# Mean over the rows of an 8192 x 8192 matrix: one add in halves, two groups at double width, and another first block for TensorE

## The chip, the cores and the metric

The kernel runs on one core of a Trainium2 chip. The metric is the device time of one execution in microseconds (us); of several runs the median is given. A profiled execution also has a span, which is the stretch of time that the trace covers; the time is somewhat longer than the span.

A core has engines that run side by side, each with its own queue of instructions: TensorE (in the profile PE, its weight loads PEld), VectorE (DVE), ScalarE (ACT), GpSimd (POOL) and SyncE (SP). Transfers are made by 16 DMA engines, to which an instruction of some engine's queue hands the work (such an instruction has a q behind the engine's name: SPq, ACTq). Engines wait for one another and for transfers by semaphores.

## The reference

```python
def setup_inputs():
    return {"x": np.random.randn(8192, 8192).astype(np.float32)}

def reference(x):
    return np.mean(x, axis=0)
```

268.4 MB are read, and 8192 sums, scaled by 1/8192, are written: 32 KB.

## The kernel before

The 8192 rows are taken as G = 64 groups of 128 rows; a group fills the 128 partitions with 8192 columns each (4 MB). The kernel has six such buffers in `bufs`: buffers 0 to 3 take loads in turn, buffer 4 is `both` and buffer 5 is `acc`, the accumulator. A "block" is F = 512 columns, so a group has 16 blocks.

**Loads.** All are issued by SyncE in a fixed order (L54), each when its buffer is free: 2 blocks of group 60 into `early`, groups 0 to 3 into buffers 0 to 3 in one transfer, groups 4 and 5 into `both` and `acc`, 4 blocks of group 63 into `early`, and then, from group 6 on, two groups in one transfer of 8 MB, in turn into buffers 0 and 1 and into 2 and 3. (`load_rows` with n groups takes n neighbouring rows to one partition; the sum over rows doesn't mind.) After group 59 come 14 blocks of group 60, all of 61 and 62, and group 63 in four parts: blocks 4 to 7, blocks 0 to 3, the columns B to Z, and the columns A to B. A is block 12, Z the end of block 15, and B lies 640 columns behind A.

**VectorE's adds** (L74, helper `add`). The first two are of double width, 128 x 16384: buffers 2 and 3 += buffers 0 and 1, then buffers 4 and 5 += buffers 2 and 3. Then `acc` += `both`. From there the loop takes two groups a step (g = 6, 8, ..., 58): `both` = one loaded buffer + the other, which frees these two for the next load, and `acc` += `both`. Behind the loop, `acc` takes blocks 0 to 13 of group 60 in one add of 7168 columns, and blocks 12 to 15 of group 61 in an add of 2048.

An add that needs a transfer doesn't wait for it alone: a no-op on ScalarE or GpSimd (L77) waits for the transfer and for the add ahead, and the add waits for the no-op. Which of the two engines has the no-op follows from the number of adds so far: `len(adds) % 8 > 1` gives ScalarE, else GpSimd. A warm-up copy on ScalarE (L95), with the table load that goes with it, stands behind the three first adds in the program, and has no no-op ahead of it on ScalarE.

**GpSimd** adds the two `early` pieces into `acc` behind the steps g = 24 and 32 (L107); the next add into `acc` waits for that through a no-op. At the end it adds the last blocks of group 62 into `acc`, in two parts (L122).

**TensorE** (L149) sums over the 128 partitions, by a matmul with a matrix of ones scaled by 1/8192, 32 columns wide. Four blocks lie in the four column groups of the array, and their sums in four quarters of a PSUM bank; three banks hold blocks 0 to 3, 4 to 7 and 8 to 11, and `most` and `last` hold the columns B to Z and A to B. Each block of float32 shows as two matmul records in the trace. The order is that in which `sums` was filled: `r61` (group 61) blocks 0 to 11, `acc` blocks 0 to 11, `r62` blocks 0 to 11, `r63` blocks 4 to 7, `most` from `acc`, `r63` blocks 0 to 3, `last` from `acc`, `most` and `last` from `r63`.

**The end.** ScalarE copies the banks (L163) and VectorE copies `last` (L179); five stores (L166) on SyncE and ScalarE write the result.

The two places of the order that the change touches:

```python
    for lo, hi, loaded in [(0, 14, 14), (12, 16, 16)]:
        row = bufs[:, (g + 2) % 4, :]
        dma = load(row[:, :loaded * F], rows(g)[:, :loaded * F])
        cols = slice(lo * F, hi * F)
        add(acc[:, cols], acc[:, cols], row[:, cols], [dma])
        g += 1
...
    blocks(r61, 0, 12)
    blocks(acc, 0, 12)
    blocks(r62, 0, 12)
```

Of the kernel before, what the change touches and what calls it, by code (L numbers as in the profile page):

```python
# [9 lines left out]
def kernel(  # L10
# [5 lines left out]
    nc = tc.nc  # L16
# [3 lines left out]
    F = 512  # L20
# [9 lines left out]
    bufs = sb.tile([P, U, N], f32, name="bufs")  # L30
    both = bufs[:, U - 2, :]
    acc = bufs[:, U - 1, :]
# [20 lines left out]
    def load(dst, src):  # L53
        ins = tc.keep_in_program_order(nc.sync.dma_start(out=dst, in_=src)).ins  # L54
        k = len(loads)
        over = loads[k - 8:k - 6] if k >= 8 and k % 2 == 0 else []
        tc.declare_no_dep(ins, group="loads", keep=over, reason="the reader of the buffer waited")
        for o in over:
            tc.add_manual_dep(ins, o.name, sync, reason="covers the next load too")
        tc.add_to_no_dep_group("loads", ins)  # L60
        loads.append(ins)
        return ins

    def rows(g, n=1):
        return x[g * P:(g + n) * P, :]

    def load_rows(g, u, n):
        return load(bufs[:, u:u + n, :], rows(g, n).rearrange("(p j) c -> p j c", j=n))
# [2 lines left out]

    def add(dst, a, b, dmas):

        ins = nc.vector.tensor_add(out=dst, in0=a, in1=b).ins  # L74
        if dmas and adds:
            waiter = nc.scalar if len(adds) % 8 > 1 else nc.gpsimd
            nop = joins[waiter] = tc.keep_in_program_order(waiter.nop()).ins  # L77
            for o in dmas + adds[-1:]:
                tc.add_manual_dep(nop, o.name, sync, reason="the no-op waits")
            for group in ("loads", "adds"):  # L80
                tc.declare_no_dep(ins, group=group, reason="the no-op waited")
            tc.add_manual_dep(ins, nop.name, sync, reason="waits for both at once")
        elif adds:
            tc.declare_no_dep(ins, group="loads", reason="the add ahead waited")
        tc.declare_no_dep(ins, group="early", reason="the no-op waited, or the add behind it")
        tc.add_to_no_dep_group("adds", ins)
        adds.append(ins)

    load(early[:, 4 * F:], rows(G - 4)[:, 14 * F:])
    first, second = load_rows(0, 0, 4), load_rows(4, 4, 2)  # L90
    load(early[:, :4 * F], rows(G - 1)[:, 8 * F:12 * F])
    add(bufs[:, 2:4, :], bufs[:, 2:4, :], bufs[:, 0:2, :], [first])
    add(bufs[:, 4:6, :], bufs[:, 4:6, :], bufs[:, 2:4, :], [second])
    add(acc, acc, both, [])
    tc.keep_in_program_order(nc.scalar.copy(out=warm[:], in_=ones[:]))  # L95
    ahead = []
    g = 6
    while g < G - 4:
        u = (g + 2) % 4
        dma = load_rows(g, u, 2)  # L100
# [3 lines left out]
        if g in (24, 32):  # L104
            lo, hi, at = (0, 4, 8) if g == 24 else (4, 6, 14)
            cols = slice(at * F, (at + hi - lo) * F)
            ins = tc.keep_in_program_order(nc.gpsimd.tensor_add(  # L107
                out=acc[:, cols], in0=acc[:, cols], in1=early[:, lo * F:hi * F])).ins
# [1 line left out]
            ahead = [ins]  # L110
        g += 2

    for lo, hi, loaded in [(0, 14, 14), (12, 16, 16)]:
        row = bufs[:, (g + 2) % 4, :]
        dma = load(row[:, :loaded * F], rows(g)[:, :loaded * F])
        cols = slice(lo * F, hi * F)
        add(acc[:, cols], acc[:, cols], row[:, cols], [dma])
        g += 1
    r61, r62, r63 = [bufs[:, (g + 1 + j) % 4, :] for j in range(3)]
    load(r62, rows(g))  # L120
    for cols in [slice(B, Z), slice(A, B)]:
        joined = tc.keep_in_program_order(nc.gpsimd.tensor_add(  # L122
            out=acc[:, cols], in0=acc[:, cols], in1=r62[:, cols])).ins
# [6 lines left out]
    def blocks(row, lo, hi):  # L130
        for i in range(lo, hi):
            sums.append((banks[i // 4], i % 4, row[:, i * F:(i + 1) * F]))

    def spread(dst, row, lo, hi):
        n = (hi - lo) // 4
        for q in range(4):
            sums.append((dst, q, row[:, lo + q * n:lo + (q + 1) * n]))

    blocks(r61, 0, 12)
    blocks(acc, 0, 12)  # L140
    blocks(r62, 0, 12)
    blocks(r63, 4, 8)
    spread(most, acc, B, Z)
# [4 lines left out]
    for n, (dst, q, cols) in enumerate(sums):  # L148
        summed = tc.keep_in_program_order(nc.tensor.matmul(  # L149
            out=dst[32 * q:32 * q + 32, :],  # L150
# [71 lines left out]
```

## Time and profile before

| | |
|---|---|
| three runs | 627.96, 629.09 and 629.38 us; median 629.09 |
| profiled execution | 628.06 us |
| its span | 626.1 us |
| VectorE busy | 525.6 us, 60 instructions |
| of these 55 adds of 128 x 8192 | 8744 ns each |
| 2 adds of 128 x 16384 | 17226 ns each |
| the add of 128 x 7168 and that of 128 x 2048 | 7624 and 2292 ns |
| TensorE busy | 15.5 us, 120 records |
| read from HBM | 268.44 MB, 429 GB/s over the span |

All times inside the profile are us from the start of the span. "L74" is line 74 of the kernel. The chain of waits is the work that ended last, followed back from the last instruction: start, duration, engine, tile and line. In a row of instructions, what stands in brackets is the idle time of the engine ahead of them, and who ended it. The windows view gives the busy time of each engine in a stretch, then the clock that TensorE was granted (1.00 is full speed), the mean share of the 16 DMA engines, and GB/s; a DMA packet is counted whole in the window in which it starts, so that a share over 1 can stand beside one of 0.

### The profile page before, as it was taken

The page shows a single profiled execution, that of the slowest core. Times are in us where ns is not written, and L with a number is a line of the kernel's source. Part 1 is how long each engine was busy: PE and PEld are TensorE (multiplying, and loading weights), DVE is VectorE, ACT ScalarE, POOL GpSimd, SP SyncE. Part 2 cuts the span into 40 slices and gives each one's busy share as a digit, 9 for nine tenths or more (in the row PEclk, how much of TensorE's full clock was granted, in tenths as well). Part 3 has the DMA queues.
Part 4 walks back from the last instruction along what each step waited for, and adds up shares of the span by engine and source line. Part 5 has one row for each costly group of instructions (what it writes and reads, how often), then busy time and mean ns, then how long its engine had stood idle before and what let it go on. Part 6 is the DMA issues. An engine that isn't in the chain of part 4 may idle for free.

```text
span 626.1 us, 465 instructions
## 1 busy us (share of the span) xinstructions
PE 15.5 (2%) x120; PEld 4.3 (1%) x120; DVE 525.6 (84%) x60; ACT 3.7 (1%) x6; POOL 12.1 (2%) x10
## 2 busy tenths in 40 slices
PE   0000000000000000000000000000000000000036
PEld 0000000000000000000000000000000000000002
DVE  0028999999888998889998889888898888998892
ACT  0000000000000000000000000000000000000001
POOL 0000000000000000020000100000000000000003
PEclk9999999999999999999999999999999999999998
DMA  9999999999999999999999999999999999999997
GB/s 377 461 402 429 442 469 402 469 402 469 402 469 402 465 406 456 414 419 452 406 465 402 469 402 469 402 469 402 469 402 469 402 465 406 431 440 410 427 435 305
DMA packets 5642, 268.50 MB, mean 429 GB/s; under 512 B 628, under 2 KB 636, under 8 KB 1032
## 3 DMA queue, kind: packets, MB, share of 16 engines
q1 hardware_dynamic: 5624, 268.46, 99.2%
q8 instruction: 1, 0.02, 0.0%
q10 hardware_dynamic: 16, 0.01, 0.0%
q14 instruction: 1, 0.01, 0.0%
HBM read 268.44 MB, written 0.03 MB: 429 GB/s over the span
## 4 chain that ended last, share of the span: by engine, by line
DMA 57%; DVE 31%; another core or an unknown queue 10%; PE 2%; issue 0%; ACTq 0%; POOL 0%; POOLq 0%
DMA bufs<-in_x_dram 57%; DVE bufs L74 31%; PE bank L149 1%; PE most L149 0%; PE last L149 0%; ACTq L77 0%; DVE tail L179 0%; POOL ready L40 0%; POOL ones L37 0%; POOLq L77 0%; POOLq L206 0%
## 5 line engine op out<-in xcount | busy, mean ns | idle before, releaser
L74 DVE TENSOR_TENSOR bufs<-bufs 128x8192 f32<-128x8192 f32 (+3 forms) x59 | 525.3, 8903 | 89.6 <-DMA bufs<-in_x_dram 43.1
L149 PE MATMUL bank<-bufs,ones 128*32 128x512 f32 x88 | 13.7, 779 | 607.8 <-DMA bufs<-in_x_dram 605.6
L107 POOL TENSOR_TENSOR bufs<-bufs,early 128x2048 f32<-128x2048 f32 (+1 forms) x2 | 6.8, 3415 | 347.7 <-DVE bufs L74 347.7
L122 POOL TENSOR_TENSOR bufs<-bufs 128x1408 f32<-128x1408 f32 (+1 forms) x2 | 4.7, 2372 | 259.8 <-DMA bufs<-in_x_dram 259.8
L149 PEld LDWEIGHTS bank<-bufs,ones 128*32 128x32 f32 x88 | 3.5, 137 | 616.7 <-issue 613.3
L179 DVE COPY tail<-last 128x160 f32<-128x160 f32 x1 | 0.3, 325 | 8.4 <-PE last L149 8.4
L163 ACT COPY bufs<-bank 128x512 f32<-128x512 f32 x3 | 1.8, 585 | 618.9 <-PE bank L149 618.9
L149 PE MATMUL most<-bufs,ones 128*32 128x352 f32 x16 | 1.5, 459 | 0.0
L95 ACT ACT_TABLE_LOAD x1 | 1.3, 1283 | 0.7 <-PEq L206 0.7
L149 PE MATMUL last<-bufs,ones 128*32 128x160 f32 x16 | 0.9, 305 | 0.0
L163 ACT COPY bufs<-most 128x352 f32<-128x352 f32 x1 | 0.5, 452 | 0.0
L149 PEld LDWEIGHTS most<-bufs,ones 128*32 128x32 f32 x16 | 0.4, 109 | 0.7 <-issue 0.6
L149 PEld LDWEIGHTS last<-bufs,ones 128*32 128x32 f32 x16 | 0.4, 109 | 1.2 <-DMA bufs<-in_x_dram 0.6
L95 ACT COPY warm<-ones 128x32 f32<-128x32 f32 x1 | 0.2, 218 | 0.0
L40 POOL TENSOR_TENSOR ready<-ones 128x1 f32<-128x1 f32 x1 | 0.2, 193 | 0.1
L37 POOL MEMSET ones<- 128x32 f32 x1 | 0.1, 124 | 0.3 <-POOLq L206 0.3
L206 POOL MEMSET const-float32-0.0<- 128x1 f32 x1 | 0.1, 98 | 0.2 <-issue 0.2
L206 POOL MEMSET const-bfloat16-1.0<- 128x1 bf16 x1 | 0.1, 101 | 0.0
L206 POOL MEMSET const-uint8-127<- 128x1 uint8 x1 | 0.1, 101 | 0.0
L206 POOL MEMSET const-float32-1.0<- 128x1 f32 x1 | 0.1, 98 | 0.0
## 6 DMA issues: line engine op xcount, KB each, us to landing
bufs<-in_x_dram SPq DMA_DIRECT2D x2, 4096.0 KB
bufs<-in_x_dram SPq DMA_DIRECT2D x1, 3584.0 KB
bufs<-in_x_dram SPq DMA_DIRECT2D x2, 1024.0 KB, 23.3
early<-in_x_dram SPq DMA_DIRECT2D x1, 1024.0 KB, 62.7
bufs<-in_x_dram SPq DMA_DIRECT2D x1, 704.0 KB, 24.5
early<-in_x_dram SPq DMA_DIRECT2D x1, 512.0 KB
bufs<-in_x_dram SPq DMA_DIRECT2D x29, 29.9
bufs<-in_x_dram SPq DMA_DIRECT2D x1, 320.0 KB, 24.8
```

What stands on the lines that cost most here:

```text
L37: nc.gpsimd.memset(ones[:], 1.0 / M)
L40: nc.gpsimd.tensor_add(out=ready[:], in0=ones[:, 0:1], in1=ones[:, 1:2]))
L74: ins = nc.vector.tensor_add(out=dst, in0=a, in1=b).ins
L95: tc.keep_in_program_order(nc.scalar.copy(out=warm[:], in_=ones[:]))
L107: ins = tc.keep_in_program_order(nc.gpsimd.tensor_add(out=acc[:, cols], in0=acc[:, cols], in1=early[:, lo * F:hi * F])).ins
L122: joined = tc.keep_in_program_order(nc.gpsimd.tensor_add(out=acc[:, cols], in0=acc[:, cols], in1=r62[:, cols])).ins
L149: summed = tc.keep_in_program_order(nc.tensor.matmul(out=dst[32 * q:32 * q + 32, :], lhsT=ones[:], rhs=cols, start=all((d is dst, k) != (T ...
L163: return tc.keep_in_program_order(nc.scalar.copy(out=dst, in_=src)).ins
L179: ended = nc.vector.tensor_copy(out=tail[:], in_=last[:]).ins
L206: nc = _bacc.Bacc("TRN2", target_bir_lowering=False, num_devices=1)
```

## The change

Three things change. Groups 6 and 7, which lie in buffers 0 and 1, are no longer the first step of the loop: they are added at double width onto buffers 4 and 5 by one add, ahead of the add of `both` into `acc`; the loop begins with group 8. The add of group 60's blocks 0 to 13 becomes two of 3584 columns, blocks 0 to 6 and 7 to 13. TensorE's order begins with blocks 0 to 6 of `acc`, then takes `r61`, then blocks 7 to 11 of `acc`. VectorE's adds are now kept in program order. The number of adds stays 59, and in the loop each step's first add has an even number instead of an odd one. All loads keep their order and sizes. The no-op for groups 6 and 7 stands ahead of the warm-up copy and its table load on ScalarE; the no-ops behind the two `early` adds of GpSimd move from GpSimd to ScalarE.

```diff
     def add(dst, a, b, dmas):
 
-        ins = nc.vector.tensor_add(out=dst, in0=a, in1=b).ins
+        ins = tc.keep_in_program_order(nc.vector.tensor_add(out=dst, in0=a, in1=b)).ins
         if dmas and adds:
             waiter = nc.scalar if len(adds) % 8 > 1 else nc.gpsimd
             nop = joins[waiter] = tc.keep_in_program_order(waiter.nop()).ins
...
     add(bufs[:, 2:4, :], bufs[:, 2:4, :], bufs[:, 0:2, :], [first])
     add(bufs[:, 4:6, :], bufs[:, 4:6, :], bufs[:, 2:4, :], [second])
+    add(bufs[:, 4:6, :], bufs[:, 4:6, :], bufs[:, 0:2, :], [load_rows(6, 0, 2)])
     add(acc, acc, both, [])
     tc.keep_in_program_order(nc.scalar.copy(out=warm[:], in_=ones[:]))
     ahead = []
-    g = 6
+    g = 8
     while g < G - 4:
         u = (g + 2) % 4
         dma = load_rows(g, u, 2)
...
-    for lo, hi, loaded in [(0, 14, 14), (12, 16, 16)]:
+    for parts, loaded in [([(0, 7), (7, 14)], 14), ([(12, 16)], 16)]:
         row = bufs[:, (g + 2) % 4, :]
-        dma = load(row[:, :loaded * F], rows(g)[:, :loaded * F])
-        cols = slice(lo * F, hi * F)
-        add(acc[:, cols], acc[:, cols], row[:, cols], [dma])
+        dmas = [load(row[:, :loaded * F], rows(g)[:, :loaded * F])]
+        for lo, hi in parts:
+            cols = slice(lo * F, hi * F)
+            add(acc[:, cols], acc[:, cols], row[:, cols], dmas)
+            dmas = []
         g += 1
...
+    blocks(acc, 0, 7)
     blocks(r61, 0, 12)
-    blocks(acc, 0, 12)
+    blocks(acc, 7, 12)
     blocks(r62, 0, 12)
     blocks(r63, 4, 8)
```

## The prediction

> **What bounds the kernel now.** I read the page first: busy shares, slices, queues.
>
> ```profile
> PE 15.5 (2%) x120; PEld 4.3 (1%) x120; DVE 525.6 (84%) x60; ACT 3.7 (1%) x6; POOL 12.1 (2%) x10
> DMA  9999999999999999999999999999999999999997
> q1 hardware_dynamic: 5624, 268.46, 99.2%
> ```
>
> The queue of the loads is busy for 99.2% of the span. VectorE (DVE), at 84%, has slack, and the chain of waits shows how much:
>
> ```profile
> 62.40 0.04 POOLq L77
> ...
> 62.46 17.24 DVE bufs L74
> ...
> 79.72 8.70 DVE bufs L74
> ...
> 88.51 8.70 DVE bufs L74
> ...
> 161.58 0.04 ACTq L77
> ...
> 200.28 0.03 ACTq L77
> ```
>
> From 161.58 on a landing releases VectorE, every 38.70 us for two pairs of groups: 19.35 us a pair, against 2 x 8.70 us of adds. Counting back in steps of 19.35 from 161.58, groups 8 and 9 land at 103.53 and groups 6 and 7 at 84.18. (Forwards: groups 4 and 5 had landed at 62.40, the 1 MB of `early` behind them is an eighth of a pair, 2.42, and 62.40 + 2.42 + 19.35 = 84.17.) So no load was late, from the first on. What can change the time is a load issued too late, or work behind the last landing. For the second, the end of the chain and TensorE's timeline:
>
> ```profile
> 604.88 7.63 DVE bufs L74
> ...
> 612.56 7.91 PE bank L149 x56
> ...
> 622.19 0.59 PE most L149 x8
> ...
> 622.01 0.77 PE L149 MATMUL most<-bufs,ones 128*32 128x352 f32 x8
> 622.75 0.11 PEld L149 LDWEIGHTS last<-bufs,ones 128*32 128x32 f32 x2 [0.61 <-DMA bufs<-in_x_dram]
> ```
>
> The chain goes through the add of group 60 and TensorE, but the last row says that TensorE's last weights waited for a transfer, until 622.75. The `most` blocks ahead, started at 622.01 and taking 0.59 by the chain, were through at 622.60. So the last landing sets the end, and TensorE is 0.15 us short of setting it. From 622.75 to 626.1 stay 3.35 us that the change doesn't touch.
>
> **The change, part by part.** The tail first.
>
> VectorE's half add: the 7168-wide add takes 7.624 us and the 2048-wide one 2.292, so an element per partition costs 5.332 / 5120 = 1.041 ns and 3584 cost 2.292 + 1536 x 0.001041 = 3.89. Started at 604.88, the first half ends at 608.77; the second, 0.02 behind it as in the chain, at 612.68, 0.17 later than today. The 2048-wide add then ends near 615.07; GpSimd, which follows, is held by the landing of group 62 until 615.45, so 0.38 us of cover takes the 0.17; without it GpSimd's first add would move 0.17 for matmuls that come 3 us behind it.
>
> TensorE: a block of 512 is two matmul records, and four blocks run side by side; I call four records a pass. By the timeline's weight loads a pass takes 0.85 us at first (606.43, 607.28, 608.13) and 0.43 later (617.28, 617.71, 618.14). The granted clock by stretches:
>
> ```profile
> 606.27:609.68 3.41, 3.41 (x20) 0.92 (x16) 3.41 (x1) 0.00 (x0) 0.00 (x0) 1.00 0.91 394
> 609.68:613.09 3.41, 1.24 (x16) 0.24 (x12) 3.31 (x2) 0.00 (x0) 0.00 (x0) 1.00 0.87 375
> 613.09:616.50 3.41, 3.41 (x24) 0.87 (x20) 1.80 (x1) 0.00 (x0) 1.05 (x1) 0.50 1.00 423
> 616.50:619.90 3.40, 3.40 (x40) 1.01 (x36) 0.00 (x0) 0.22 (x1) 3.40 (x2) 1.00 0.99 410
> ```
>
> (Columns: stretch, length, busy PE, PEld, DVE, ACT, POOL, granted clock, DMA.) A stretch of 3.41 us that TensorE filled is followed by full clock, one with 1.24 of 3.41 busy by half clock. (In the first stretch the passes of 0.85 say half clock, though the column has 1.00.) Today's 14 passes from 612.56 to the end of `r63`'s first part, at full clock 14 x 0.43 = 6.02, and half of 3.41 lost to the half clock, 1.71, give 620.29, where the timeline has the next matmuls. Changed: TensorE starts at 608.77 + 0.06 = 608.83, not at 605.60. Seven blocks make two groups (4 + 3), `r61` three, and blocks 7 and 8 to 11 two more, as block 7 stands alone: 14 passes where today there are 12. With the eight of `r62` and `r63` that is 22 x 0.43 = 9.46. If the stretches lie as today, half clock lasts from 608.83 to 613.09 and costs 2.13: the same point is reached at 620.42, 0.13 later. The waiting 0.15 us takes that. Block 7 isn't reached before 608.83 + 10 x 0.43 = 613.13, behind the second half's 612.68. Sum of the tail: 0.0.
>
> Where will the boundaries lie? In quarter-microsecond windows the granted clock falls at 613.09 and rises at 616.50; neither these nor 609.68 fits TensorE's starts at 605.60 and 612.56, so the rows don't tell how they lie to a start at 608.83.
>
> The Trainium skill, "TensorE: Matmul & The Clock Gate", Part 1, says outright that the window of 3.4 us is free-running and not started by the kernel. The 3.41 above agrees; by the page the 0.13 would be a draw, anywhere between the ends that follow.
>
> By the rows: full clock comes at the end of a filled stretch, so at best the half clock lasts 1.24 us of part-filled stretch (more than 1.24 busy is needed), costing 0.62, and at worst 2 x 3.41 = 6.82, costing 3.41. The point today at 620.29 then lies between 618.91 and 621.70; behind it come 0.59, 0.86, 0.27 and 0.59 (chain), so the last blocks could start between 621.2 and 624.0, against 622.75 for the last landing: the tail costs 0.0 to +1.3, and nothing up to 4.3 us of half clock. The runs of before have the same uncertainty, with a gap from 610.4 to 612.56. I take 0.0, the alignment of the one execution that is shown.
>
> The start. Groups 6 and 7 were added alone, at 88.51, and their buffers were free at 97.21. One double-width add takes 17.23, not 2 x 8.70 + 0.02: VectorE is spared 0.19. But it stands ahead of the add into the accumulator and must wait for groups 6 and 7: VectorE now idles from 79.70 to 84.18 + 0.06 = 84.24, ends at 101.47, and the buffers come free 4.26 us later. The load of groups 10 and 11, issued at 97.23, goes out at 101.49. Queued behind the waiting add are the accumulator's adds: groups 8 and 9 are added at 110.2 to 118.9 (106.0 to 114.7 today), their buffers' next load still 3.5 us ahead of its need. VectorE gains 1.93 us per pair and is level by 181. When does the transfer of groups 8 and 9 let go? Packets are counted at their start:
>
> ```profile
> 102.50:102.75 0.25, 0.00 (x0) 0.00 (x0) 0.25 (x1) 0.00 (x0) 0.00 (x0) 1.00 1.22 524
> 102.75:103.00 0.25, 0.00 (x0) 0.00 (x0) 0.25 (x1) 0.00 (x0) 0.00 (x0) 1.00 7.89 3408
> 103.00:103.25 0.25, 0.00 (x0) 0.00 (x0) 0.25 (x1) 0.00 (x0) 0.00 (x0) 1.00 0.61 262
> 1.75:2.00 0.25, 0.00 (x0) 0.00 (x0) 0.00 (x0) 0.25 (x1) 0.00 (x0) 1.00 1.56 147
> 3.50:3.75 0.25, 0.00 (x0) 0.00 (x0) 0.00 (x0) 0.00 (x0) 0.00 (x0) 1.00 3.80 1622
> ```
>
> Groups 10 and 11 begin at 102.5 to 103.25, most near 102.88: 1.39 us after the new issue (5.65 us after the old). An issue's lead is seen at the kernel's start only: the first went out at 0.74 and moved data from 1.75, 1.0 us; the second, at 1.19, had its large packets from about 3.6, 2.4 us, though behind the first. By 1.0 nothing is lost, by 2.4 it is 1.0 us, and all that follows is late by it. I take 1.5, nearer to the first row because the second contains another transfer: +0.1.
>
> The skill's "DMA: Bandwidth & Descriptors", Latency and other measured facts, speaks against the change: it gives HBM access as 0.2 us on average and 2 us at high load. No run here shows a load issued to a nearly empty queue mid-kernel. An estimate by that page alone, 1.0 + 1.8 = 2.8 us of lead, would lose 1.4 us.
>
> At no cost: ScalarE's table load and copy (1.28 + 0.22) move behind the no-op at 84.2; ScalarE's next no-op is needed at 110.2. Without that cover VectorE would wait 1.5. The no-ops of groups 26 and 34 move from GpSimd to ScalarE: 0.04 against 0.05 in the chain, under VectorE's 1.93 of idle. SP issues the same loads in the same order.
>
> Sum: 0.0 + 0.1 against the profiled execution, 628.06 with 2 us around its 626.1; the median, 1.03 higher, becomes 629.2.
>
> **Rivals.** No change, 629.2, is the forecast.
>
> Slower: TensorE sets the end. It starts 3.23 us later and does two passes more, so when a boundary falls just ahead of 608.83 and nearly a filled stretch is needed, the last blocks are ready 1.3 us behind the last landing: 630.4. For: the end is 0.15 us from TensorE. Against: it takes most of a second stretch at half clock. It costs from 4.3 us of half clock on, and the full price needs 6.8.
>
> Slower or inside 0.2%: the queue runs dry before groups 10 and 11. It costs from 1.4 us of lead on; at 2.4 us 630.1, at 2.7 us 630.4. For: the margin shrinks from 5.65 us to 1.4. Against: the row of 1.0.
>
> Faster: the median of before is 1.03 over the profiled execution. If that is a late TensorE (the gap behind 610.4 can leave two stretches short of busy, so 5 to 6.8 us at half clock behind 612.56 where today it is 3.41, some 1.3 us more), the unbroken run of matmuls removes it: 629.09 - 1.3 = 627.8. For: the gap. Against: one execution is shown, and there the gap costs nothing.
>
> That the change doesn't do what it says: TensorE is to be busy without a break, yet it begins 3.23 us later, on an add rather than on a landing. If the pause is only moved ahead, nothing comes of it; the time is the forecast's.
>
> **How the numbers follow.** The forecast has 0.53; TensorE late 0.17; the dry queue 0.12, half of it over 0.2%; the faster rival 0.18. A measurement of this kernel can tell about 0.2%, 1.26 us, from no change. So slower is 0.17 + 0.06 = 0.23, same 0.53 + 0.06 = 0.59, faster 0.18. The range leaves out about half of each outer case: from 627.7, just under the faster rival, to 630.6, just over TensorE late. The forecast's own range is 628.5 to 630.2: 0.7 below by the scatter of the three runs (half of 1.4), above by the dry queue's 1.0.
>
> **What would show it.** Groups 10 and 11 landing at 122.9 (steps right) or up to 124 (queue dry); DMA slices without a hole after 101.5; halves of 3.89 us; TensorE's first matmul at 608.8 and no gap until `r63`; the last weights still waiting for a DMA. Wrong if VectorE's wait moves ahead of a landing after 181, or if the time behind the last landing isn't 3.35 us.

## The result and the profile after

The changed kernel takes 631.25 us (median of 8 runs, 630.38 to 633.04) against 629.12 for the one before: ratio 1.0040, 95% interval 1.0027 to 1.0054. It is slower by 2.1 us, and the forecast of no change was wrong. The profiled execution took 631.26 us, its span is 629.3, 3.2 us longer than the 626.1 of before.

First the page of the changed kernel, its busy line and the queue of the loads:

```profile
PE 14.3 (2%) x120; PEld 4.3 (1%) x120; DVE 525.5 (84%) x60; ACT 3.7 (1%) x6; POOL 12.1 (2%) x10
q1 hardware_dynamic: 5624, 268.46, 98.9%
```

Engines do the same work as before, and the queue is busy for 98.9% of the span instead of 99.2%. 0.3% of 629 us is 1.9 us of 16 engines, so the loads are the place to look. The chain of waits of the changed kernel (start, duration, what):

```profile
60.41 23.85 DMA bufs<-in_x_dram
...
84.32 17.24 DVE bufs L74
...
101.58 8.70 DVE bufs L74
...
136.61 28.16 DMA bufs<-in_x_dram
164.77 0.03 ACTq L77
...
203.47 0.03 ACTq L77
...
608.11 3.90 DVE bufs L74
...
612.14 11.49 PE bank L153 x80
```

The double-width add starts at 84.32, on the landing of groups 6 and 7, and ends at 101.56 (84.24 and 101.47 were computed). Then the landing that releases VectorE stands at 164.77 where it stood at 161.58: all of the 3.2 us is lost by 165 us, and nothing behind it: 203.47 is 38.70 later, the same step as before, and the add of group 60 starts at 608.11 instead of 604.88, 3.23 later. The end keeps its length too. TensorE's timeline and SyncE's issues in the changed kernel:

```profile
101.57 0.33 SPq L54 DMA_DIRECT2D bufs<-in_x_dram  x1
625.97 0.13 PEld L153 LDWEIGHTS last<-bufs,ones 128*32 128x32 f32 x4 [0.63 <-DMA bufs<-in_x_dram]
```

The last weights wait for a DMA again, 3.22 us later than at 622.75; from there to the end are 3.3 us (3.35 before). Now the place: the load of groups 10 and 11 goes out at 101.57. The windows view of before, then of the changed kernel; the last two columns are the share of the DMA engines and GB/s, counted where a packet starts:

```profile
102.50:103.00 0.50, 0.00 (x0) 0.00 (x0) 0.50 (x1) 0.00 (x0) 0.00 (x0) 1.00 4.55 1966
103.00:103.50 0.50, 0.00 (x0) 0.00 (x0) 0.50 (x1) 0.00 (x0) 0.00 (x0) 1.00 0.30 131
103.50:104.00 0.50, 0.00 (x0) 0.00 (x0) 0.50 (x1) 0.00 (x0) 0.00 (x0) 1.00 0.00 0
```

```profile
102.50:103.00 0.50, 0.00 (x0) 0.00 (x0) 0.50 (x1) 0.00 (x0) 0.00 (x0) 1.00 3.32 1180
103.00:103.50 0.50, 0.00 (x0) 0.00 (x0) 0.50 (x1) 0.00 (x0) 0.00 (x0) 1.00 1.08 393
103.50:104.00 0.50, 0.00 (x0) 0.00 (x0) 0.50 (x1) 0.00 (x0) 0.00 (x0) 1.00 0.00 0
104.00:104.50 0.50, 0.00 (x0) 0.00 (x0) 0.50 (x1) 0.00 (x0) 0.00 (x0) 1.00 0.39 131
104.50:105.00 0.50, 0.00 (x0) 0.00 (x0) 0.50 (x1) 0.00 (x0) 0.00 (x0) 1.00 0.76 262
105.50:106.00 0.50, 0.00 (x0) 0.00 (x0) 0.50 (x1) 0.00 (x0) 0.00 (x0) 1.00 4.37 1573
```

Such rows can be counted. A large packet is 65.5 KB, so 1966 GB/s for 0.5 us are 15 packets, and 131 are one: before, all 16 engines begin the new load within a microsecond. Their mean duration is share x 16 x 0.5 / packets: 4.55 x 8 / 15 = 2.43 us. In the changed kernel 1180 + 393 make 12 packets in the same microsecond; the other engines begin 1.3 us and more later, one between 104.0 and 104.5, two in the next half microsecond, the fourth from 105.5 on (nothing starts between 105.0 and 105.5). And the 12 take (3.32 + 1.08) x 8 / 12 = 2.93 us each instead of 2.43; so do the packets that start from 105.5 to 106 (4.37 x 8 / 12 = 2.91). The first of these, alone in a narrow window, is the fourth late engine's, as no packet of the 12 has ended by then:

```profile
105.50:105.58 0.08, 0.00 (x0) 0.00 (x0) 0.08 (x1) 0.00 (x0) 0.00 (x0) 1.00 2.42 819
```

It takes 2.42 x 16 x 0.08 = 3.10 us. So 12 engines lose some 1.0 us over two packets. The four late ones lose 1.3 us and more by idling and some 0.6 on the packet that follows; the last of them lets go of the load before between 102.8 and 103.2, by the trace's packets, and starts at 105.5, which makes 2.3 to 2.7 us, and 0.7 on its packet: 3.0 to 3.4, the 3.2 of the landing. Every load is divided evenly among the 16, and its landing waits for the last of them.

### The profile page after: what moved, and what is told of

The parts are those of the page before. It is cut to its first block, busy times and chain, and to the rows that moved or that the text cites. A ratio compares the mean times of both kernels' runs of the same rounds, so it can differ in the third digit from the quotient of the medians.

```text
span 629.3 us, 465 instructions
## 1 busy us (share of the span) xinstructions
PE 14.3 (2%) x120; PEld 4.3 (1%) x120; DVE 525.5 (84%) x60; ACT 3.7 (1%) x6; POOL 12.1 (2%) x10
## 3 DMA queue, kind: packets, MB, share of 16 engines
q1 hardware_dynamic: 5624, 268.46, 98.9%
## 4 chain that ended last, share of the span: by engine, by line
DMA 67%; DVE 30%; PE 2%; issue 0%; ACTq 0%; SPq 0%; POOLq 0%
DMA bufs<-in_x_dram 67%; DVE bufs L74 30%; PE bank L153 2%; PE most L153 0%; PE last L153 0%; ACTq L77 0%; SPq L54 0%; DVE tail L183 0%; POOLq L77 0%
## 5 line engine op out<-in xcount | busy, mean ns | idle before, releaser
L96 ACT ACT_TABLE_LOAD x1 | 1.3, 1283 | 84.3 <-DMA bufs<-in_x_dram 84.3
```

## The experiments

**The change in two halves.** First the tail alone, in the kernel before:

```diff
+    blocks(acc, 0, 7)
     blocks(r61, 0, 12)
-    blocks(acc, 0, 12)
+    blocks(acc, 7, 12)
```

with group 60 in two adds, as in the change.

> Before, with the halves of group 60 and TensorE's new order alone; groups 6 and 7 as before. Theory (the transfers ran dry before groups 10 and 11, and that is the whole loss): the time of before, ratio 0.999 to 1.001, last weights waiting for the last landing near 622.7. Rival (TensorE, which starts later and does two passes more, makes the loss): 1.003 to 1.005, without a wait of the last weights for a DMA.

Then the start alone:

```diff
+    add(bufs[:, 4:6, :], bufs[:, 4:6, :], bufs[:, 0:2, :], [load_rows(6, 0, 2)])
     add(acc, acc, both, [])
...
-    g = 6
+    g = 8
```

> Before, with groups 6 and 7 added at double width alone (the no-op for group 61 is kept on ScalarE). Theory: the whole loss, ratio 1.003 to 1.005, and the landing that releases VectorE near 164.8 instead of 161.6. Rival (the loss is at the tail): 0.999 to 1.001.

The tail alone: 628.87 us, ratio 0.9995 (0.9987 to 1.0003). Its last weights wait for a DMA, 0.7 us later than in the kernel before; that is taken up below:

```profile
623.44 0.16 PEld L152 LDWEIGHTS last<-bufs,ones 128*32 128x32 f32 x8 [0.61 <-DMA bufs<-in_x_dram]
```

The start alone: 630.97, ratio 1.0027 (1.0018 to 1.0037), a little under what was expected. The chain of waits with the start alone:

```profile
84.25 17.24 DVE bufs L74
...
136.55 27.86 DMA bufs<-in_x_dram
164.41 0.04 ACTq L77
...
203.47 0.03 ACTq L77
```

Its landing of 164.41 is 2.8 us late, and the next, at 203.47, is 3.2 late, as in the changed kernel: the loss is at the start, and the rival that TensorE makes it falls.

**Keep the add, take away the empty queue.** In the changed kernel a small load goes behind groups 8 and 9 instead of to the head:

```diff
-    load(early[:, 4 * F:], rows(G - 4)[:, 14 * F:])
...
         dma = load_rows(g, u, 2)
+        if g == 8:
+            load(early[:, 4 * F:], rows(G - 4)[:, 14 * F:])
```

> The changed kernel, with the 0.5 MB load of group 60 moved from the head of the loads to behind groups 8 and 9. The double-width add stays; groups 6 and 7 land 1.2 us sooner, so the load of groups 10 and 11 is issued near 100.3, and the queue holds the same bytes until 102.9: a lead of 2.5 us instead of 1.3. Theory (only the empty queue costs): the time of before, 0.998 to 1.001, if 2.5 us of lead is enough; part of the loss if not. Rival (the double-width add costs by itself, by the later adds behind it): 1.003 to 1.005 as in the changed kernel.

628.64 us, ratio 0.9997 (0.9987 to 1.0007), with everything else of the change in it. Its windows at the same place:

```profile
102.50:103.00 0.50, 0.00 (x0) 0.00 (x0) 0.50 (x1) 0.00 (x0) 0.00 (x0) 1.00 2.98 1270
103.00:103.50 0.50, 0.00 (x0) 0.00 (x0) 0.50 (x1) 0.00 (x0) 0.00 (x0) 1.00 2.81 1212
```

By the view of its chain the release at the place of 161.58 is at 161.87. The double-width add by itself costs nothing.

**The late issue without the change.** The kernel before, with an add on a dead tile, of four sizes, ahead of the add of groups 6 and 7 (and the adds kept in program order, as in the change):

```diff
+        if g == 6:
+            tc.keep_in_program_order(nc.vector.tensor_add(
+                out=both[:, :4000], in0=both[:, :4000], in1=both[:, :4000]))
         add(both, bufs[:, u, :], bufs[:, u + 1, :], [dma])
```

> Before, with one extra add of 4000 columns in place on the dead tile both, 4.3 us, ahead of the add of groups 6 and 7. Nothing else of the change is in it; the buffers come free at 101.5 as in the changed kernel. Theory (the late issue costs, by whatever delays it): ratio 1.003 to 1.005. Rival (the order or width of the adds): 0.999 to 1.001, as VectorE has slack.

> As the run with the extra add of 4000 columns, with 3500: 3.8 us, the load of groups 10 and 11 issued near 101.0, a lead of 1.9 us. It looks for the lead that is enough, between 1.4 (loss) and 2.3 (no loss). If the lead needed is that of the kernel's first load (1.0 to 1.6 us from issue to first packets): no loss, 0.999 to 1.001. If some engines get their descriptors later than that: part of the loss, 1.001 to 1.003.

> The same with 5120 columns, 5.5 us: issue near 102.6, a lead of 0.2 us, 1.2 us less than with 4000. If the loss is the lateness of the issue and nothing more, it grows by that 1.2 us, to 1.0045 (some 3.0 us). If an engine that has run dry pays a price of its own that covers the lateness, it stays near 1.003.

> The same with 7040 columns, 7.5 us: issue near 104.7, 1.8 us behind the first engine that lets go, so all 16 engines run dry. By lateness alone, counted from the run of 4000 columns: 1.8 + 3.2 = 5 us, 1.008; by a price of restarting of some 2 us for each engine on top of the gap of 1.8: 1.006 to 1.007.

The issue as the trace has it, the lead to 102.88, where most engines let go in the kernel before, and the landing that stands at 200.28 in the chain of the kernel before:

| columns | issue | lead | landing | time | ratio, interval |
|---|---|---|---|---|---|
| none (before) | 97.23 | 5.65 | 200.28 | 629.18 and 628.75 | 1 |
| 3500 | 101.18 | 1.70 | 200.89 | 629.15 | 1.0013 (1.0003 to 1.0023) |
| 4000 | 101.44 | 1.44 | 202.82 | 630.91 | 1.0026 (1.0016 to 1.0036) |
| 5120 | 102.70 | 0.18 | 202.12 | 630.55 | 1.0031 (1.0020 to 1.0041) |
| 7040 | 104.62 | -1.74 | 203.84 | 632.51 | 1.0062 (1.0048 to 1.0075) |

(4000 columns ran beside 629.18, the others beside 628.75.) The landing, from one execution each, has the loss of the loads at this place alone; the times also hold what happens later, of which two things are told below. An issue as late as that of the changed kernel costs 2.5 us at the landing, most of the changed kernel's 3.2, with none of its other edits. The loss isn't the lateness: from a lead of 1.44 to one of 0.18 the ratio hardly moves and the landing comes 0.7 us earlier; only with 7040 columns both grow. The windows of the run with 5120, then of that with 7040:

```profile
103.50:104.00 0.50, 0.00 (x0) 0.00 (x0) 0.50 (x1) 0.00 (x0) 0.00 (x0) 1.00 5.56 1835
104.00:104.50 0.50, 0.00 (x0) 0.00 (x0) 0.50 (x1) 0.00 (x0) 0.00 (x0) 1.00 0.71 262
```

```profile
105.00:105.50 0.50, 0.00 (x0) 0.00 (x0) 0.50 (x1) 0.00 (x0) 0.00 (x0) 1.00 0.00 0
105.50:106.00 0.50, 0.00 (x0) 0.00 (x0) 0.50 (x1) 0.00 (x0) 0.00 (x0) 1.00 5.95 1966
106.00:106.50 0.50, 0.00 (x0) 0.00 (x0) 0.50 (x1) 0.00 (x0) 0.00 (x0) 1.00 0.36 131
```

In both, all 16 engines have run dry and start together. With 7040 columns they do so 0.9 to 1.9 us after the issue at 104.62, and the first packets take 5.95 x 8 / 15 = 3.17 us. Taking 105.8 for their start, they wait 2.9 us and lose 0.74 on the first packet: 3.7, and the landing is 3.56 late. With 5120, taking 103.8, they wait 0.9 and lose 0.7 (6.27 x 8 / 16 = 3.14 us a packet): 1.6, and the landing is 1.84 late. So where all run dry the price is the wait and slow first packets. Where only some do, those come late: in the changed kernel up to 3.9 us behind the issue, while the other 12 had begun by 1.9. In the profiled executions this was the dearer case, 2.5 and 3.2 us with leads of 1.44 and 1.31, against 1.8 with one of 0.18. Why some engines get their work that late, and why the first packets are slow, wasn't found.

**The empty queue in another place.** In the changed kernel the 1 MB load of group 63 behind groups 8 and 9, in place of the small one:

> The changed kernel, with the 1 MB load of group 63 (not the 0.5 MB of group 60) moved to behind groups 8 and 9. The load of groups 10 and 11 then has a lead near 3.8 us, but that of groups 6 and 7, issued at 60.4 when the first add ends, loses the 2.4 us of transfer that stood ahead of it, and has 1.4 us. Theory (an empty queue costs wherever it comes): the loss is back, 1.002 to 1.005, with the late engines from 62 us on and none at 103. Rival (the place or the double add costs): as with the other early load, 0.999 to 1.001.

629.62 us, ratio 1.0014 (1.0005 to 1.0023); its times run from 628.54 to 630.22. The profile is of the fastest of these. Its windows, where groups 6 and 7 begin:

```profile
61.50:62.00 0.50, 0.00 (x0) 0.00 (x0) 0.00 (x0) 0.00 (x0) 0.00 (x0) 1.00 5.20 1966
62.00:62.50 0.50, 0.00 (x0) 0.00 (x0) 0.12 (x1) 0.00 (x0) 0.00 (x0) 1.00 0.37 131
```

No engine is late here, but the first packets take 5.20 x 8 / 15 = 2.77 us instead of 2.42, and the release at the place of 161.58 is at 162.06. By the times the loss is partly back, at a place that the change didn't touch; how large it is differs from one execution to the next, and late engines at this place were not seen.

**More lead.** The small load and half of the other behind groups 6 and 7:

```diff
+    load(early[:, :2 * F], rows(G - 1)[:, 8 * F:10 * F])
...
     add(bufs[:, 4:6, :], bufs[:, 4:6, :], bufs[:, 0:2, :], [load_rows(6, 0, 2)])
+    load(early[:, 2 * F:4 * F], rows(G - 1)[:, 10 * F:12 * F])
+    load(early[:, 4 * F:], rows(G - 4)[:, 14 * F:])
```

> The changed kernel, with the 0.5 MB load of group 60 and the second half of the 1 MB load of group 63 (now two loads of 0.5 MB) moved to behind groups 6 and 7. The load of groups 10 and 11 then has a lead near 4 us, that of groups 6 and 7 one of 2.6. If the empty queue is the whole loss, and the tail's change by itself takes away the upper group of times of the kernel before (a late last store, 1.1 us): 628.0 to 628.6, below both kernels, ratio 0.998 to 0.9995. If the tail's change brings nothing: 0.9995 to 1.0005, with two groups of times as before.

Neither came: 630.13 us, ratio 1.0025 (1.0013 to 1.0036), and in its chain the release at the place of 161.58 is at 162.96. Its windows, where groups 6 and 7 begin:

```profile
62.00:62.50 0.50, 0.00 (x0) 0.00 (x0) 0.50 (x1) 0.00 (x0) 0.00 (x0) 1.00 2.16 819
62.50:63.00 0.50, 0.00 (x0) 0.00 (x0) 0.50 (x1) 0.00 (x0) 0.00 (x0) 1.00 0.72 262
```

The slow packets are back at this place: 262 GB/s for 0.5 us are two packets, and they take 0.72 x 8 / 2 = 2.88 us each. The load was issued at 59.30, at least 2.2 us ahead. So 2.2 us and more wasn't enough here, with two more loads issued right behind, where 2.3 was enough above. The lead that is needed is no single number; 5.65 us lost nothing.

**What hid in the tail's result.** The tail alone came out level, yet the view of its chain has one long step (from 480 us on), and so has another profile of it:

```profile
479.90 30.66 DMA bufs<-in_x_dram
...
519.34 29.92 DMA bufs<-in_x_dram
```

It has 60 adds instead of 59. The kernel before with one more add on the dead tile, of 32 columns:

> Before, with one more instruction on VectorE alone: an add of 32 columns in place on the dead tile both, ahead of the add of groups 6 and 7; its own time is under 0.2 us and VectorE has slack. If 60 adds instead of 59 bring a fetch of instructions in the middle of the loads, which takes a DMA engine from them: the transfers 0.4 to 0.8 us later from about 470 or 485 us on, a packet of another queue there, and 1.0007 to 1.0013 (less if the end is shorter for it). If the count of instructions means nothing: 0.9995 to 1.0005 and no such packet; then the landing that was 0.7 us late in the run of the tail alone came from the tail's edit.

628.82 us, ratio 1.0002 (0.9994 to 1.0011), and in its chain:

```profile
441.26 30.57 DMA bufs<-in_x_dram
471.83 0.03 ACTq L77
...
480.61 29.93 DMA bufs<-in_x_dram
```

0.65 us are lost in one step (30.57 against 29.92), and its trace has an 8 KB packet of an instruction queue at 465.5, the tail's trace one at 484.9; before and after have none between 20 and 600 us. In the windows view of the run with the add of 32 columns it is the part of 925.5 KB that 14 packets of 65.5 leave over:

```profile
465.50:466.00 0.50, 0.00 (x0) 0.00 (x0) 0.50 (x1) 0.00 (x0) 0.00 (x0) 1.00 4.36 1851
```

All seven profiles with 60 adds (the four sizes of the dead add among them) have such a packet between 465 and 486 us, and none of the eleven with 59. In six of the seven a step of the chain near it is 0.45 to 0.8 us longer; with 4000 columns none is. So one add more on VectorE brings the fetch and, mostly, this loss, and the change as a whole avoids that: the double-width add saves the instruction that the halves add. With 60 adds in both, the ratio to the kernel before is 0.9995 with the tail's edit and 1.0002 without it, which these intervals don't tell apart: the tail's edit brings nothing that could be measured. That the times of 60 adds are no longer than those of before has a reason in the next part: in the seven the packet at the end, which makes the upper group of times, is missing.

**The two groups of times.** The kernel before mostly runs near 628.1 or near 629.1 (a few of its times, near 630.3 to 630.6, stay unexplained). It was profiled again, three times (629.13, 628.05 and 629.38 us), and the tail alone once (629.0):

> Before, unchanged, for another profile: its times lie in groups near 628.1 and 629.1. If the upper group is a TensorE that ends late (the rival by which the change would have been faster), a profile of it has the last landing near 622.7 as now and its last matmuls some 1 us behind it, without a wait for a DMA. If it is the transfers, the last landing itself is 1 us later.

> The tail's change alone, for another profile: its times lie between 628.6 and 629.3, without the two groups. If TensorE's end made the groups, its last matmuls wait for a DMA here; if the transfers did, its last landing lies between those of the two groups.

Two of the profiles, of 629.13 and 629.38 us, are of the upper group. Of the first (span 627.2) the waits of SyncE's queue, and TensorE's and VectorE's timeline:

```profile
SPq L217 <- DMA out_dram<-tail: 1.8, 1, 1.8
622.00 0.80 PE L149 MATMUL most<-bufs,ones 128*32 128x352 f32 x8 [0.40 <-DMA bufs<-in_x_dram]
623.34 0.32 DVE L179 COPY tail<-last 128x160 f32<-128x160 f32 x1 [8.42 <-PE last L149]
```

The last copy starts at 623.34, as in the profile of before (623.30), and TensorE waits for the transfers: it is early, not late. What is longer is the wait for the last store, 1.8 us instead of 0.4. What differs ahead of that is that TensorE and so the store of blocks 0 to 3 were early (issued at 622.01 instead of 622.89), and with it VectorE's last no-op, which waits for that store. In the same trace the 8 KB packet of an instruction queue, which comes at 625.72 in the profile of before, starts near 625.0, in the middle of the last store. The windows of before, then of this profile (164 GB/s for 0.05 us are 8.2 KB):

```profile
625.70:625.75 0.05, 0.00 (x0) 0.00 (x0) 0.00 (x0) 0.00 (x0) 0.00 (x0) 1.00 0.64 164
```

```profile
625.00:625.05 0.05, 0.00 (x0) 0.00 (x0) 0.00 (x0) 0.00 (x0) 0.00 (x0) 1.00 0.52 164
```

The other two profiles fit: with the store issued at 622.09 the packet starts at 625.03, in the last store, and the time is 629.38; with 622.49 it starts at 625.35, behind it, and the time is 628.05. In the second profile of the tail alone the last weights wait for a DMA until 623.62, 0.8 to 0.9 us later than in either group: its times lie between the groups by the fetch in the middle and not by TensorE. VectorE's last no-op tied to a later store, in the kernel before and in the changed kernel with the small load behind groups 8 and 9:

```diff
-    tc.add_manual_dep(hold, s0.name, sync, reason="VectorE ends late")
+    tc.add_manual_dep(hold, s3.name, sync, reason="VectorE ends late")
```

(s3 is the store of the columns B to Z.)

> Before, with VectorE's last no-op waiting for the store of the columns B to Z, issued at 623.33, instead of that of blocks 0 to 3, issued at 622.89 in the profiled execution and at 622.01 in the upper group of times. If the upper group comes from VectorE leaving before the last store has gone: the group near 629.1 is gone, median 628.0 to 628.4, ratio 0.9982 to 0.9992, below both kernels. If the upper group has another cause (TensorE, or the loads): two groups as before, 0.9995 to 1.0005.

> The changed kernel with the 0.5 MB load of group 60 behind groups 8 and 9, and with that later wait of VectorE's last no-op. If both losses are taken away: as the other run of this pair, 628.0 to 628.5, as the tail's change brings nothing by itself. If the lead of 2.3 us is too short in some executions: a part of the times 1 us or more above, and a median over that of the other.

628.37 us, with 11 of 12 times between 628.18 and 628.79 and one at 630.64; ratio 0.9994 (0.9984 to 1.0004). The changed kernel: 628.63, all 11 times between 628.34 and 628.84; ratio 0.9996 (0.9988 to 1.0005); without the later wait four of its 12 times lay from 629.5 to 630.5. The upper group is gone in both (9 of the 23 runs of before beside them lie from 629.06 to 629.58), so VectorE's early end is what makes it. Both intervals hold 1, so neither is shown to beat the kernel before; both lie below the changed one.

## Why the prediction was wrong

The step that failed is the last of the start, "By 1.0 nothing is lost, by 2.4 it is 1.0 us, and all that follows is late by it. I take 1.5 ...: +0.1." The place, the mechanism and the times up to it were right: VectorE idle until 84.3, the add done at 101.5 (computed 101.47), the load issued at 101.49 (measured 101.57). The term of +0.1 measured 3.2 in the profiled execution, 2.1 in the medians; the rival of the dry queue, 630.1 to 630.4, had the cause and 0.12 of the chance. Three things were wrong in the price of +0.1. The lead was taken from the kernel's first load, as one number for all engines: 12 kept to it, four didn't. That first load already showed the other half of the price. The 147 GB/s of its first row are nine packets of 4.1 KB, which took 1.56 x 16 x 0.25 / 9 = 0.69 us each; by this row, a little later, 22 packets take 0.88 x 4 / 22 = 0.16:

```profile
3.25:3.50 0.25, 0.00 (x0) 0.00 (x0) 0.00 (x0) 0.00 (x0) 0.00 (x0) 1.00 0.88 360
```

The other two errors are these. A lack of lead was priced as lateness, one for one above 1.39 us; the sizes show that the price sets in near 1.7 us of lead (landing 0.6 us late) and is 2.5 us at 1.44 (1.7 in the medians). And it was a mean over engines, where a landing waits for the slowest, which never catches up, as the queue is full again for the rest of the loads.

"VectorE is spared 0.19" was right (17.24 us) and worth nothing. VectorE waits for a landing again at 164.77, sooner than "level by 181", but only because that landing is itself 3.2 us late.

The tail, 0.0: right in its sum, in part by luck. The halves take 3.90 (computed 3.89). But TensorE's passes were miscounted: 80 records are 20 passes, not 22, so the group of three and block 7 share passes with their neighbours. From 612.14 at 0.43 a pass and half clock until 617.87 (weight loads 0.85 apart up to there and 0.43 behind it, though the column of the granted clock shows 1.00), 20 x 0.43 + 5.73 / 2 = 11.5, the 11.49 of the chain. By 22 it would have been 12.3. The prediction had 9.46 + 2.13 = 11.59: its two passes too many (0.86 us) and a half clock of 4.26 us instead of 5.73 (0.73 us) nearly cancel. The weight loads around the step:

```profile
616.38 0.22 PEld L153 LDWEIGHTS bank<-bufs,ones 128*32 128x32 f32 x3 [0.63 <-issue]
617.24 0.22 PEld L153 LDWEIGHTS bank<-bufs,ones 128*32 128x32 f32 x5 [0.64 <-issue]
617.87 0.13 PEld L153 LDWEIGHTS bank<-bufs,ones 128*32 128x32 f32 x4 [0.41 <-issue]
618.30 0.13 PEld L153 LDWEIGHTS bank<-bufs,ones 128*32 128x32 f32 x4 [0.30 <-issue]
```

The rival that TensorE sets the end didn't come: with 5.7 us of half clock the last weights still waited 0.63 us for a DMA. By the prediction's sum 4.3 us would have been the limit; the two passes fewer, 0.86 us, are worth 1.7 us more of half clock.

The faster rival was wrong in its ground: the upper group of times isn't a late TensorE but a late last store, in executions in which TensorE is early. ScalarE's table load and the moved no-ops cost nothing, as said: they stand in the run with the early load moved as well, at 0.9997.

The Trainium skill, "DMA: Bandwidth & Descriptors", Latency and other measured facts, with its 2 us of HBM access at high load, pointed the right way; the estimate drawn from it, a loss of 1.4 us, was nearer than the +0.1, though no run here tells whether HBM access is the reason.

## What to carry to other kernels

Where the transfers are the bound, ask of each edit on another engine when it frees a buffer, and how far ahead of the queue's last packet the next load then goes out; here 5.65 us was safe, and 1.44 cost 2.5 us in the profiled execution and 1.7 in the medians, once and for good. Price a queue that runs dry by its slowest engine, not by the mean. Count instructions too: one more add moved a fetch of instructions from the end into the loads, where it took 0.7 us, and without its cause the tail's edit could have been blamed.

## What the runs showed of the hardware

Some of the 16 engines can get the work of a new load much later than the others, when they have run dry and the others haven't: 3.9 us after the issue, against 0.9 to 1.9. The first packets of a load issued with a lead of 1.4 us or less take 2.8 to 3.2 us instead of 2.42, in the changed kernel twice for each of 12 engines; in one run they were as slow with 2.2 us of lead and more. A fetch of 8 KB of instructions delayed the loads by 0.45 to 0.8 us in six of seven profiles, and at the end, where it met the last store of 2.5 KB, the kernel by about a microsecond.
